# Hybrid RWKV-7 and Conformer layer on one core: the scan phase in the order of its source instead of the build's order

## The chip, the cores and the metric

The kernel runs on one core of a Trainium2 chip. The metric is the device time of one execution in microseconds (us). A kernel's time is the median of its runs; a profiled execution, taken by the hardware profiler, gives the trace from which all rows below come. The engines are TensorE (PE, with its weight loads listed apart as PEld), VectorE (DVE), ScalarE (ACT), GpSimd (POOL) and SyncE (SP), whose queue (SPq) issues the DMA transfers.

## What is computed

One layer works on 2048 latent tokens of 1024 channels, after a prefix of 256 context tokens. The normed and modulated input goes through one wide projection `w_in` and then through two branches, an RWKV-7 time mixing (16 heads of size 64, scanned forward and backward) and a Conformer convolution (31 taps), which are gated, added and projected:

```python
h = rmsnorm(x, norm_w) * (1.0 + scale[:, None]) + shift[:, None]
p = h @ w_in
prep = rwkv_prepare(rk, w0, w2, a0, a2, k_k, k_a)
y_sum, _, _ = rwkv_scans(prep, sc_f, sc_b)        # s = s*w + (s a) b + v k, forward and backward
y_a = rwkv_readout(y_sum, prep, r_k, lnx_w, lnx_b) * silu(g_a)
y_b = conformer_conv(glu, conv_w, conv_b, cln_w, cln_b) * silu(g_b)
merged = sigmoid(m_a) * (y_a @ w_proj_a) + sigmoid(m_b) * (y_b @ w_proj_b)
x_new = x + gate[:, None] * (merged @ w_out)
```

The layer's output goes through a last RMSNorm with `final_norm_w`.

## The kernel before, in words

The kernel has three phases. **Phase 1** (to about 1650 us of the span) makes `h`, projects the RWKV columns and part of the gates, and turns the recurrence into chunks of 64 tokens: for each chunk it stores small matrices (the inverse in `Tt`, the arrays `ar`, `bk`, `v`) in DRAM. Its last work is an `invert` on DVE, PE and ACT (L468 to L503).

The **scan phase** (L772 to the end of the loop over `g`) runs 8 pairs of heads x 9 steps x 4 chunks = 288 chunks, each for both directions. `chunk` (L989) is a chain: two matmuls `px` from the state `SV` and `arz` (PE), the copy `xs` (ACT), two matmuls `px` from `xs` and `Tt` (PE), the copy `UV` (ACT), `psy` from `UV` and `BK` (PE), and the next state `SV` (DVE, from `psy` and `pre`, which POOL makes). `outputs` (the matmuls `py`, then `y`) belongs to the chunk before. `prep` (L858) works for the next step: it loads `bk`, `ar`, `vvz`, `Tt`, and in pieces between the chunks it transposes (`pbk`, then `BK` on ACT; `pvt`, then `SV` and `UV` on ACT) and multiplies `psc` (PE), of which DVE makes `arz` and `sc`. `pbk`, `pvt`, the two `psc` and the readout's `pc` and `pv` share one PSUM pool, `pC`, of two buffers. `readout` normalizes finished rows and uses `Ln` and `Exp` on ACT.

Into the waits of this chain the source emits **filler**: `fill_gen` projects the columns of the gates and of the GLU in matmuls of 128x512 into `pg`, the products of the convolution run on DVE as chains of multiply-adds (`conv_gen`: `accq`, then `acc`), and, from chunk 236 on, `conv_branch` normalizes and projects (`pp`). How many fillers are emitted is decided by `until`, `conv_steps` and `pull`, from a model of the engines' clocks that the class `Clocked` (L789) keeps; it wraps PE, ACT and DVE, and so nearly all instructions of the scan carry the line of its call, L822. A filler's weights come through `load_w1` and `load_w2`: `load_w1` loads 512 KB of float32 into `wf` (L183; one buffer) and has ACT square it into `wjk` with the sum in `wss`; `load_w2` sums over partitions (`pf`, PE), makes a power of two from it (`p2f`, `p2t`, `p2x`, `p2s`, seven small instructions of DVE), and casts to `whi` (ACT) and `wlo` (DVE). In `fill_gen` the second half of one load, `second()`, and the first half of the next, `first()`, are called one after the other:

```python
def ahead(npr):
    if not w2:
        second()
    for _ in range(npr):
        yield from chore(prs.pop(0))
    first()
    yield
```

The **last phase** merges the branches, projects with `w_out` and writes the output.

In the whole kernel before, the build decides the order of instructions on every engine, and the order differs from that in which the source emits them. Each engine executes its instructions in the order that it gets. The parts of the code that the change touches are printed here.

Of the kernel before, what the change touches and what calls it, by code (L numbers as in the profile page):

```python
# [79 lines left out]
def kernel(ctx, tc, x, xT, cc, pp, w_in, w_mod, w_lora, w_pa, w_pb, w_out, fnw, bmg, out):  # L80
# [688 lines left out]
    s1.close()  # L769

    clk = dict(pe=0.0, dve=0.0, act=0.0, mode=0)
# [676 lines left out]
            pass  # L1451
    while "first" not in c_:
        next(cb, None)
    sb.close()

    c1 = pool(ctx, "c1", 1, "right")
# [146 lines left out]
```

## Time and profile before

| what | value |
|---|---|
| time, median of 3 runs | 4116.91 us (4113.39 to 4122.94) |
| the profiled execution | 4115.85 us |
| its span, first to last instruction | 4114.1 us |
| mean granted TensorE clock in it (share of full) | 0.966 |
| PE busy | 3802.2 us, 92% |
| DVE busy | 2950.5 us, 72% |
| ACT busy | 2181.7 us, 53% |

Busy time is time in which an engine executes; for PE it is no proof of full speed, since a slower clock makes each matmul longer. In a row such as `[1.30 <-ACT xs L822]` the engine had been idle for 1.30 us before the instruction, and what ended the idle time was ACT's instruction that writes `xs`. `128x512` are partitions x elements. A float32 matmul shows in the trace as two instructions, so that `x4` in a row of the timeline are two of the source. The rows of a timeline put several equal neighbours together (`x4`), with the time from the first's start to the last's end.

### The profile page before, as it was taken

Reading aid. Unit: us, or ns where it says so; the run is one execution under the profiler, and the core shown is the slowest. Engines: PE = TensorE matmul, PEld = TensorE weight load, DVE = VectorE, ACT = ScalarE, POOL = GpSimd, SP = SyncE. Lnnn points to the kernel's source line nnn. Section 1 sums busy time; section 2 is a strip of 40 time slices with the busy share of each in tenths; the row PEclk is TensorE's granted clock in tenths of the full one; section 3 lists DMA queues with packets and bytes.
Section 4 is the critical chain, followed back from the end, with each engine's and each line's share of the span. In section 5 each row is a group of like instructions: output and inputs, shape, how many; then the busy total and the mean of one; then the engine's idle time right before and its main releaser. Section 6 shows DMA issues by size and latency. Waiting matters only on the chain. (4 is left out here: it accounts for less than half of the span.)

```text
span 4114.1 us, 78249 instructions
## 1 busy us (share of the span) xinstructions
PE 3802.2 (92%) x29008; PEld 2254.8 (55%) x29008; DVE 2950.5 (72%) x7226; ACT 2181.7 (53%) x4356; POOL 356.8 (9%) x874
## 2 busy tenths in 40 slices
PE   7999999999999897999999999999999989898999
PEld 3444444444444443676666666666676655564444
DVE  5578788687778868768696869977765566754644
ACT  5666665666666554445445454455446546544522
POOL 0000000000000000111111111111111100010000
PEclk9999999999999999999999999999999999999999
DMA  5344443444444333444444433434554555546532
GB/s 205 127 165 144 157 162 134 140 149 157 146 150 162 134 137 115 92 81 115 88 107 96 113 87 82 124 86 104 118 125 116 139 160 126 148 107 203 163 101 75
DMA packets 586116, 528.68 MB, mean 129 GB/s; under 512 B 375044, under 2 KB 439940, under 8 KB 585224
## 3 DMA queue, kind: packets, MB, share of 16 engines
q1 hardware_dynamic: 585736, 523.68, 44.2%
q8 instruction: 231, 3.78, 0.4%
q14 instruction: 149, 1.22, 0.1%
HBM read 298.01 MB, written 196.35 MB: 120 GB/s over the span
## 5 line engine op out<-in xcount | busy, mean ns | idle before, releaser
L822 DVE SCALAR_TENSOR_TENSOR SV<-psy,PL,pre 64x64 f32<-64x64 f32 x1120 | 315.8, 282 | 187.7 <-PE psy L822 168.1
L1013 POOL TENSOR_SCALAR pre<-SV,PL 128x128 f32<-128x128 f32 x560 | 290.0, 518 | 1780.1 <-DVE SV L822 1708.0
L822 PE MATMUL pg<-hH,whi 128*128 128x512 f16 x864 | 336.1, 389 | 5.7 <-ACT whi L822 4.0
L822 PE MATMUL pg<-hH,wlo 128*128 128x512 f16 x864 | 335.6, 388 | 0.4 <-DVE wlo L822 0.3
L822 PE MATMUL pg<-hL,whi 128*128 128x512 f16 x864 | 335.8, 389 | 0.0
L822 DVE SCALAR_TENSOR_TENSOR acc<-z,cw,acc 128x512 f32<-128x512 f32 x464 | 331.7, 757 | 2.7
L212 PE MATMUL pg<-hH,whi 128*128 128x512 f16 x832 | 319.0, 385 | 4.7 <-ACT hH L282 4.5
L213 PE MATMUL pg<-hL,whi 128*128 128x512 f16 x832 | 319.7, 384 | 0.1
L214 PE MATMUL pg<-hH,wlo 128*128 128x512 f16 x832 | 319.2, 384 | 0.0
L822 ACT ACTIVATE xs<-px 128x256 f32<-128x256 f32 x288 | 109.3, 380 | 383.1 <-PE px L822 381.5
L822 PE MATMUL psc<-arz,bk 64*128 64x128 f32 (+1 forms) x2304 | 259.5, 293 | 14.7 <-ACT UV L822 7.1
L822 ACT ACTIVATE UV<-px 64x128 f32<-64x128 f32 x576 | 156.1, 271 | 211.7 <-PE px L822 207.0
L363 PE MATMUL pg<-hH,whi 128*128 128x512 f16 x672 | 259.9, 387 | 2.4 <-ACT whi L203 2.4
L363 PE MATMUL pg<-hL,whi 128*128 128x512 f16 x672 | 259.4, 386 | 0.0
L363 PE MATMUL pg<-hH,wlo 128*128 128x512 f16 x672 | 258.7, 385 | 0.7 <-DVE wlo L204 0.7
L822 PEld LDWEIGHTS <-whi 128*128 128x128 f16 x1728 | 172.8, 101 | 149.7 <-issue 20.2
L822 PEld LDWEIGHTS psc<-arz,bk 64*128 64x128 f32 x2304 | 211.7, 192 | 65.9 <-issue 13.3
L822 PE MATMUL px<-SV,arz 128*128 128x128 f32 x1152 | 222.8, 297 | 24.8 <-DVE SV L822 22.9
L822 PEld LDWEIGHTS px<-SV,arz 128*128 128x128 f32 x1152 | 181.9, 195 | 84.5 <-issue 29.3
L822 PE MATMUL psy<-UV,BK 128*128 128x128 f32 x1120 | 200.4, 300 | 25.6 <-ACT UV L822 23.2
L822 PE MATMUL px<-xs,Tt 128*128 128x128 f32 x1152 | 194.7, 292 | 29.4 <-ACT xs L822 28.3
L822 DVE TENSOR_TENSOR arz<-psc,msk 64x256 f32<-64x256 f32 x288 | 120.5, 419 | 140.7 <-PE psc L822 137.1
(376 smaller groups left out, 8704.2 us busy)
## 6 DMA issues: line engine op xcount, KB each, us to landing
wf<-in_w_in_dram SPq DMA_DIRECT2D x74, 512.0 KB, 3.8
arz<-arD SPq DMA_DIRECT2D x144, 256.0 KB, 4.9
bkD<-bk SPq DMA_DIRECT2D x64, 512.0 KB, 2.7
arD<-ar SPq DMA_DIRECT2D x64, 512.0 KB, 3.5
bk<-bkD SPq DMA_DIRECT2D x72, 256.0 KB, 3.8
bk<-bkD SPq DMA_DIRECT2D x144, 128.0 KB, 3.9
vvz<-vD SPq DMA_DIRECT2D x144, 128.0 KB, 2.9
lt<-loD SPq DMA_DIRECT2D x32, 512.0 KB, 4.9
```

The costliest lines, as they stand in the source:

```text
L212: PE.matmul(ps, whi[:, k, :], xhi(k), start=(k == 0), stop=False)
L213: PE.matmul(ps, whi[:, k, :], xlo(k), start=False, stop=False)
L214: PE.matmul(ps, wlo[:, k, :], xhi(k), start=False, stop=(k == NK - 1))
L363: PE.matmul(ps, wt[a][:, k, :], b[:, k, o:o + 512], start=(m == 0), stop=(m == 23))
L822: return fn(*a, **kw)
L1013: G.tensor_scalar(pr, SV[:, d, c, :], pl, 1.0, op0=ALU.mult, op1=ALU.mult)
```

## The change

From the start of the scan phase to the last chunk, the instructions of PE, ACT and DVE are issued in the order in which the source emits them. SP and POOL stay in the build's order, and so do all engines before and after. No instruction is added or removed by the source.

```diff
@@ -769,6 +769,9 @@
     s1.close()


+    order = ctx.enter_context(ExitStack())
+    order.enter_context(tc.manual_schedule(engines={mybir.EngineType.PE, mybir.EngineType.Activation, mybir.EngineType.DVE}))
+

@@ -1451,6 +1454,7 @@
     while "first" not in c_:
         next(cb, None)
+    order.close()
     sb.close()
```

Lines behind the first insertion move by 3: the line L822 of the call in `Clocked` is L825 in the changed kernel. What the change moves is shown at three places, by listings of the order in which an engine gets its instructions; numbers behind a name tell buffers apart.

ACT at a weight load in the middle of the scan (`f` belongs to a gate of the filler, `xs` and `UV<-px` to a chunk, `UV<-pvt` to `prep`), before:

```order
L822 ACTIVATE f_25514<-pg,un 128x512
L822 ACTIVATE xs<-px 128x256
L822 ACTIVATE UV<-pvt 64x4x64 x2
L822 ACTIVATE whi<-wf,p2s 128x1024
L822 ACTIVATE UV<-px 64x2x64 x2
L822 ACTIVATE wjk,wss<-wf 128x1024
L822 ACTIVATE xs<-px 128x256
```

and now, at the same load:

```order
L825 ACTIVATE f_25516<-pg,un 128x512
L825 ACTIVATE whi<-wf,p2s 128x1024
L825 ACTIVATE wjk,wss<-wf 128x1024
L825 ACTIVATE xs<-px 128x256
L825 ACTIVATE UV<-px 64x2x64 x2
L825 ACTIVATE UV<-pvt 64x4x64 x2
L825 ACTIVATE xs<-px 128x256
```

`wjk`, which reads the next tile's `wf`, now follows `whi` directly, and the `xs` and `UV` of the running chunk moved from ahead of them to behind them.

PE in a later chunk, where `prep` goes from `psc` of one direction to `pbk` of the next, before:

```order
L822 MATMUL px<-xs,Tt_18646 128x128 x2
L822 MATMUL psc<-arz_18649,bk 128x64 x8
L822 MATMUL psy<-UV,BK 128x128 x2
L822 LDWEIGHTS whi
L822 MATMUL pg<-hL,whi 128x512
L822 LDWEIGHTS wlo
L822 MATMUL pg<-hH,wlo 128x512
L822 LDWEIGHTS whi
L822 MATMUL pg<-hH,whi 128x512
L822 MATMUL pbk<-ident,bk 128x128 x4
L822 MATMUL pvt<-ident,vvz 128x128 x4
```

and now:

```order
L825 MATMUL px<-xs,Tt_18648 128x128 x2
L825 MATMUL psc<-arz_18651,bk 128x64 x8
L825 MATMUL pbk<-ident,bk 128x128 x2
L825 MATMUL psy<-UV,BK 128x128 x2
L825 MATMUL pbk<-ident,bk 128x128 x2
L825 MATMUL pvt<-ident,vvz 128x128 x4
L825 LDWEIGHTS whi
L825 MATMUL pg<-hL,whi 128x512
```

Two of the four `pbk` moved ahead of `psy` and directly behind `psc`, and the fillers `pg` that stood ahead of `pbk` now come after `pvt`.

ACT at the start of the scan (L588, L495 and L503 are phase 1), before:

```order
L588 ACTIVATE A_17786<-pA 32x256 x2
L822 ACTIVATE wjk,wss<-wf 128x1024
L822 ACTIVATE whi<-wf,p2s 128x1024
L822 ACTIVATE wjk,wss<-wf 128x1024
L822 ACTIVATE whi<-wf,p2s 128x1024
L822 ACTIVATE wjk,wss<-wf 128x1024
L822 ACTIVATE f_18941<-pg,un 128x512
L822 ACTIVATE whi<-wf,p2s 128x1024
L495 ACTIVATE DF<-pf 32x512 x2
L503 ACTIVATE A_17786<-pf 32x512 x2
L822 ACTIVATE wjk,wss<-wf 128x1024
```

and now, with all of phase 1 ahead of it:

```order
L825 ACTIVATE xs<-px 128x256
L825 ACTIVATE wjk,wss<-wf 128x1024
L825 ACTIVATE whi<-wf,p2s 128x1024
L825 ACTIVATE wjk,wss<-wf 128x1024
L825 ACTIVATE whi<-wf,p2s 128x1024
L825 ACTIVATE wjk,wss<-wf 128x1024
L825 ACTIVATE UV<-px 64x2x64 x2
L825 ACTIVATE xs<-px 128x256
```

The first weight loads moved from between the steps of the last `invert` to between the first chunk's `xs` and its `UV`.

## Rows read from the trace of the kernel before

**Rows 1.** The page's first part: busy time, share of the span, instructions of each engine.

```profile
PE 3802.2 (92%) x29008; PEld 2254.8 (55%) x29008; DVE 2950.5 (72%) x7226; ACT 2181.7 (53%) x4356; POOL 356.8 (9%) x874
```

**Rows 2.** Groups of instructions, 1680 to 3750 us: busy, mean ns | idle before, releaser.

```profile
L822 PE MATMUL px<-SV,arz 128*128 128x128 f32 x1148 | 222.0, 297 | 24.8 <-DVE SV L822 22.9 <-DVE arz L822 0.2
...
L822 PE MATMUL psy<-UV,BK 128*128 128x128 f32 x1120 | 200.4, 300 | 25.6 <-ACT UV L822 23.2
L822 PE MATMUL px<-xs,Tt 128*128 128x128 f32 x1152 | 194.7, 292 | 29.4 <-ACT xs L822 28.3
...
L822 PE MATMUL pbk<-ident,bk 128*128 128x128 f32 x568 | 93.6, 280 | 24.5 <-DVE sc L822 23.8 <-DVE arz L822 0.3
```

**Rows 3.** Timeline of ACT at one weight load: start, us, instruction, [idle before <-releaser].

```profile
2347.49 0.37 ACT L822 ACTIVATE xs<-px 128x256 f32<-128x256 f32 x1
...
2350.80 1.15 ACT L822 ACTIVATE whi<-wf,p2s 128x1024 f16<-128x1024 f32 x1 [2.15 <-DVE p2s L822]
2352.08 0.56 ACT L822 ACTIVATE UV<-px 64x128 f32<-64x128 f32 x2
2357.71 1.06 ACT L822 ACTIVATE wjk<-wf 128x1024 f16<-128x1024 f32 x1 [5.08 <-DMA wf<-in_w_in_dram]
```

**Rows 4.** Timelines of DVE and of SP's queue at the same load.

```profile
2351.98 1.28 DVE L822 SCALAR_TENSOR_TENSOR wlo<-wf,p2s,whi 128x1024 f16<-128x1024 f32 x1 [1.22 <-ACT whi L822]
...
2353.42 0.56 SPq L183 DMA_DIRECT2D wf<-in_w_in_dram  x1
```

**Rows 5.** Timeline of ACT at the first weight loads of the scan.

```profile
1618.83 1.15 ACT L822 ACTIVATE whi<-wf,p2s 128x1024 f16<-128x1024 f32 x1 [4.47 <-DVE p2s L822]
1625.01 1.06 ACT L822 ACTIVATE wjk<-wf 128x1024 f16<-128x1024 f32 x1 [5.04 <-DMA wf<-in_w_in_dram]
...
1629.26 1.15 ACT L822 ACTIVATE whi<-wf,p2s 128x1024 f16<-128x1024 f32 x1 [3.10 <-DVE p2s L822]
1635.28 1.06 ACT L822 ACTIVATE wjk<-wf 128x1024 f16<-128x1024 f32 x1 [4.87 <-DMA wf<-in_w_in_dram]
```

**Rows 6.** Timeline of PE at the same loads.

```profile
1614.40 0.38 PE L822 MATMUL pf<-wss,ones 128*128 128x1 f32 x2 [3.00 <-ACT wjk L822]
1626.21 0.59 PE L822 MATMUL pf<-wss,ones 128*128 128x1 f32 x2 [11.43 <-ACT wjk L822]
```

**Rows 7.** Timeline of PE at the load of rows 3.

```profile
2346.42 0.28 PE L822 MATMUL pf<-wss,ones 128*128 128x1 f32 x2
...
2351.43 0.61 PE L822 MATMUL px<-xs,Tt 128*128 128x128 f32 x4
...
2353.61 0.38 PE L822 MATMUL pg<-hL,whi 128*128 128x512 f16 x1
...
2355.77 0.71 PE L822 MATMUL px<-SV,arz 128*128 128x128 f32 x4
...
2359.32 0.71 PE L822 MATMUL px<-xs,Tt 128*128 128x128 f32 x4 [1.30 <-ACT xs L822]
```

**Rows 8.** Timeline of ACT at the first chunk of the scan.

```profile
1679.62 0.38 ACT L822 ACTIVATE xs<-px 128x256 f32<-128x256 f32 x1 [2.86 <-PE px L822]
1680.81 0.56 ACT L822 ACTIVATE UV<-px 64x128 f32<-64x128 f32 x2 [0.80 <-PE px L822]
```

**Rows 9.** The tile pbk, 1680 to 3750 us: PE's idle time before it, times.

```profile
  DVE sc L822: 23.8, 19
```

**Rows 10.** Timeline of DVE: seven conv steps of one chain, and of two.

```profile
2055.39 5.48 DVE L822 SCALAR_TENSOR_TENSOR accq<-z,cw,accq 128x512 f32<-128x512 f32 x7
...
1903.50 4.84 DVE L822 SCALAR_TENSOR_TENSOR acc<-z,cw,acc 128x512 f32<-128x512 f32 x7
```

**Rows 11.** Groups of instructions, 1680 to 3750 us: ACT's table loads.

```profile
L822 ACT ACT_TABLE_LOAD x68 | 87.2, 1283 | 1.2
```

**Rows 12.** Timeline of PE behind a long wait.

```profile
3415.70 1.22 PE L822 MATMUL px<-xs,Tt 128*128 128x128 f32 x4 [4.12 <-ACT xs L822]
```

**Rows 13.** The stretch behind it: busy us of each engine, PEclk, DMA share, GB/s.

```profile
core 0: us, PE busy (x) PEld busy (x) DVE busy (x) ACT busy (x) POOL busy (x), PEclk, DMA share, GB/s
...
3415.70:3422.40 6.70, 6.70 (x28) 4.46 (x29) 6.56 (x19) 6.66 (x13) 0.00 (x0) 0.51 0.17 33
```

## The prediction, made before the changed kernel had run

> **What bounds the kernel now.** I read the page's busy times first: TensorE (PE) works 92% of the span, VectorE (DVE) 72%, ScalarE (ACT) 53% [rows 1]. So PE sets the time, and what the change is worth is PE's idle time that it removes or adds. Then I grouped instructions by what ended the idle time before them, in the scan (1680 to 3750 us). PE's largest idle groups there are small: 29.4 us before `px<-xs,Tt`, 25.6 before `psy`, 24.8 before `px<-SV,arz`, 24.5 before `pbk` [rows 2], 104 us in 2070. The scan is a chain (px, xs, px, UV, psy, SV) with filler matmuls `pg` packed into its waits, and the build packs them well. The question is therefore whether the source's order packs as well; the order listings say where it doesn't, and the trace gives prices.
>
> **The change, part by part.** Nothing is added or removed in arithmetic; three instruction streams are ordered otherwise from the start of the scan to the last chunk. On PE the two orders are nearly the same chunk by chunk (fillers per chunk too, after the start). Five places differ.
>
> *1. Weight loads on ACT (the term that decides).* A weight tile goes `pf` (PE), the small pow2 steps and then `whi` (ACT), `wlo` (DVE), the transfer of the next `wf` (SP; one buffer, so it waits for `whi` and `wlo`), `wjk` (ACT). In the source `second()` and `first()` follow each other, so that in the new order `wjk` stands directly behind `whi` in 41 of 43 loads of the scan; the build does that in the first three and puts 1 to 12 other ACT instructions between them in the rest. Now ACT stops at `wjk` until the transfer has landed, and xs or UV of the running chunk stands behind it. At the load of the first listing, in the trace, xs of that chunk ran at 2347.49, ahead of `whi` at 2350.80; `whi` ended 2351.95, `wlo` began 2351.98 (1.28), the transfer was issued at 2353.42 (0.56), and `wjk` began 2357.71 [rows 3, 4]: 5.76 us, of which some 3.7 are the landing. How long the whole circle takes where nothing stands between `whi` and `wjk` the trace shows at the start of the scan, where the build has the source's arrangement: ACT waits 5.04 and 4.87 us for the transfer [rows 5], and from `pf` to the end of the following `wjk` there are 1614.40 to 1626.07, 11.7 us, and 1626.21 to 1636.34, 10.1 us [rows 5, 6]. With the accumulator read behind `wjk` (the next `pf` began 0.14 after it) and xs (0.37, [rows 3]), a matmul that needs xs comes some 10.6 us after `pf`. What PE has in between is fixed by the new order: counted over the 41 loads, with 0.216 us for a filler (ten from 2353.61 to 2355.77, [rows 7]) and 0.22 to 0.3 for the others, it is 5.0 us on average (1.1 to 11.1). For the load of the listing: `pf` at 2346.42, the matmul that needs xs at 2351.43 [rows 7], so 5.0 us are covered and 5.6 are not. Three of the 41 belong to the start (part 2). **38 x 5.6 = 213 us.** Ends: if half of the 3.10 us goes for which ACT waited for the pow2 steps of the second circle [rows 5], since they are no longer mixed with other DVE work, 38 x 4.1 = 156; if the circle is that of the first of the two, 38 x 7.2 = 274. I take 213, since in the second circle there is less DVE work. A part was paid already: the next `px` in the trace waited 1.30 us for xs [rows 7]; that goes into part 6.
>
> *2. The start.* The build runs 144 filler matmuls (31 us of PE) and the first three weight loads beside the last `invert` on DVE, 1614 to 1650. In the new order all of them stand behind the first px. The scan may begin earlier: first xs at 1679.62 now [rows 8], some 1664 then, as DVE is relieved of some 6 us and SP's loads move up. But ACT's new order is xs, `wjk`, `whi`, `wjk`, `whi`, `wjk`, UV: two circles at about 10 us each, so first UV at about 1687 instead of 1680.81. With 31 us of fillers to do later: 6 + 31, I take **+40** (25 if the start comes earlier, 50 if a transfer is late).
>
> *3. `pbk` right behind `psc`.* It needs a PSUM buffer that DVE frees with arz and sc. In the new order 72 `psc` groups have `pbk` next, in the old 27; elsewhere `psy` and fillers stood between. Where the wait shows in the trace it is 23.8 us in 19 cases, 1.25 each [rows 9]. 45 more x 1.25 = **56 us**; ends 0 (DVE there already) and 90 (2 us each, with a conv step of 0.78 ahead [rows 10]). `psy`, on the chain, waits behind it.
>
> *4. Conv steps on DVE.* The build mixes two independent chains, seven steps in 4.84 us; a single chain takes 5.48, so 0.69 and 0.78 a step [rows 10]. Some 460 `acc` steps: 41 us of DVE, which has 28% idle [rows 1]. I take **+20**, from 0 to 41.
>
> *5. Table loads.* 39 instead of 71 in the scan: 32 x 1.283 us [rows 11] = 41 us of ACT, most of it where xs waits. **-30**, ends 0 and -41.
> The Trainium skill (ScalarE: Activation LUTs, What ACT_TABLE_LOAD costs) puts a switch at 1283 ns and a drain of about 1380 ns: 2.66 us, and by that 85 us would go, which speaks for the change. By it the term would be some -62 and the time 4393, an estimate. The row agrees with the 1283, and no row here shows the drain, so I stay with the row.
>
> *6. Clock and catch-up.* Behind an idle of 4.12 us before a `px` [rows 12] the granted clock was 0.51 for 6.7 us [rows 13], that is the 1.2 GHz level: up to 3.3 us of PE time. With 38 new idles of that kind: 0 to 125; I take 1 us each, **+40**, as low stretches of now go where their idles go. For waits of now that the new ones swallow [rows 2]: **-30**.
>
> Sum: 40 + 213 + 56 + 20 - 30 + 40 - 30 = 309. The profiled execution took 4115.85 us, a microsecond under the median of the three runs, 4116.91: 4425 us.
>
> **The rivals.**
> (a) *Milder.* PE runs so far behind that ACT's stop costs little: transfers land in 3 us, pow2 runs at once, and a late chunk is made good with fillers. For it: 1.30 us was all that the example cost [rows 7]. Against it: in the new order no filler stands ahead of the waiting matmul beyond those counted. Loads at 2 us, 76 instead of 213, clock 10, `pbk` 25: 4116 + 40 + 76 + 10 + 25 + 20 - 30 - 30 = 4227.
> (b) *Heavier.* DVE stops too (`wlo` waits for `whi`, and arz and SV stand behind it), and every stop brings the slow clock: 274 for loads, 125 for the clock, `pbk` 56: 4116 + 40 + 274 + 125 + 56 + 20 - 30 - 30 = 4571. For it: the slow clock behind the idle shown [rows 12, 13]. Against it: idles of a microsecond are common now, and PE's mean clock is high nevertheless.
> The Trainium skill (TensorE: Matmul & The Clock Gate, What's actually happening) has the array throttled unless activity releases it; the row of that idle agrees, and by the rule every new idle threatens a slow stretch, as this rival says.
> (c) *Faster.* The build's order mixes ACT work of later chunks ahead of the chain; the source's order puts the chain first. Half of the 104 us of idle and 30 us of table loads go: 4116 - 52 - 30 + 40 = 4074, if a load costs PE nothing. It decides where a load costs PE less than (52 + 30 - 40)/38 = 1.1 us, i.e. where xs follows `pf` within 6.1 us instead of 10.6. For it: ACT is idle half of the time. Against it: `whi` (1.15), `wlo` (1.28), issue (0.56) and landing (3.7) make 6.7 alone [rows 3, 4], and twice the circle was measured at over 10 [rows 5, 6].
> (d) *Nothing happens.* The listings show all three streams changed; only a sum that cancels would give it, 4117.
>
> **How the numbers follow.** Forecast 0.52 (4310 to 4520), (a) 0.2, (b) 0.18, (c) 0.08, (d) 0.02. The range 4190 to 4580 leaves out (c), (d) and the tails of (a) and (b). About 0.2% is what a measurement of this kernel can tell from no change; slower by more than that 0.9, faster 0.08, within 0.02.
>
> **What would show it.** Right: in the changed profile ACT has some 200 us of idle before `wjk` ended by the transfer of `wf` (now 5 us in the example), xs and UV follow it, and PE's idle before `px<-xs` and `psy<-UV` grows from 55 to over 200 us; `pbk` waits for sc rise to some 80; the first chunks take 7 us each; table loads fall by 32; the mean clock falls below 0.95. Wrong: idle before `wjk` large but PE's idle not (a), DVE idle before `wlo` and a clock at 0.9 (b), or PE's idle below that of now (c).

## The result, and the profile after

The changed kernel takes 4703.58 us (median of 4 runs, 4699.69 to 4709.07), the kernel before beside it 4115.15 us: a ratio of 1.1428, 95% interval 1.1407 to 1.1449. The forecast was slower, by 309 us to 4425, with a range up to 4580. The direction was right; the loss is 588 us, nearly twice the forecast and outside the range.

The profiled execution took 4709.07 us. Its page, with the busy times that answer to [rows 1]:

```profile
span 4707.3 us, 78279 instructions
...
PE 3896.6 (83%) x29008; PEld 2334.0 (50%) x29008; DVE 3014.2 (64%) x7226; ACT 2142.0 (46%) x4324; POOL 372.4 (8%) x874
```

PE's busy time rose by 94 us (3802.2 to 3896.6) with the same 29008 matmuls, and its idle time, span less busy, from 312 to 811 us, by 499. Together that is the whole difference of the spans, 593 us. Where it lies shows in the two kernels cut at the same places of the program: the end of phase 1, the `xs` of chunk 24, of chunk 228 and of the last chunk, the end. First the kernel before (columns: busy time of each engine in the stretch, PEclk the granted clock, DMA share, GB/s):

```profile
core 0: us, PE busy (x) PEld busy (x) DVE busy (x) ACT busy (x) POOL busy (x), PEclk, DMA share, GB/s
0.00:1640.00 1640.00, 1497.14 (x14708) 711.04 (x14709) 1233.92 (x3118) 997.95 (x1602) 63.33 (x287) 0.96 0.43 149
1640.00:1811.40 171.40, 165.03 (x1289) 121.46 (x1288) 130.99 (x292) 74.46 (x198) 31.59 (x57) 1.00 0.44 89
1811.40:3253.00 1441.60, 1348.73 (x8725) 958.54 (x8724) 1096.55 (x2658) 723.41 (x1671) 210.83 (x416) 0.97 0.45 105
3253.00:3744.50 491.50, 445.86 (x2719) 306.90 (x2717) 297.20 (x733) 252.00 (x584) 51.02 (x115) 0.94 0.54 140
3744.50:4114.10 369.60, 345.42 (x1574) 156.87 (x1574) 191.87 (x428) 133.92 (x302) 0.00 (x0) 0.97 0.40 130
```

and now the changed kernel:

```profile
0.00:1640.00 1640.00, 1493.69 (x14670) 709.05 (x14670) 1230.86 (x3090) 991.05 (x1592) 63.02 (x287) 0.96 0.42 149
1640.00:1877.20 237.20, 171.21 (x1317) 127.36 (x1318) 85.19 (x241) 80.74 (x206) 23.05 (x53) 0.82 0.31 67
1877.20:3737.10 1859.90, 1427.94 (x8740) 1024.69 (x8739) 1197.67 (x2733) 694.12 (x1649) 233.81 (x420) 0.87 0.34 83
3737.10:4328.90 591.80, 454.14 (x2706) 313.75 (x2705) 308.54 (x736) 244.01 (x584) 52.55 (x114) 0.88 0.44 117
4328.90:4707.30 378.40, 349.57 (x1581) 159.12 (x1579) 191.94 (x428) 132.10 (x296) 0.00 (x0) 0.96 0.37 123
```

Phase 1 and the last phase are as they were. The start of the scan costs 66 us more (237.2 against 171.4), the 204 chunks after it 418 (1859.9 against 1441.6), chunks 228 to the last 100. In the middle stretch 79 of the 418 are busy time of the same matmuls: the granted clock fell from 0.97 to 0.87 of full. That is the level of 1.2 GHz taken more often: between 1640 us and the last chunk the clock was low in 95 stretches, 709 us together, against 23 with 143 us before.

The groups of instructions of the changed kernel's scan, with the idle time before them and what ended it, answer to [rows 2, 11]:

```profile
L825 PE MATMUL pg<-hH,whi 128*128 128x512 f16 x864 | 352.1, 407 | 61.1 <-ACT whi L825 33.2 <-ACT f L825 27.4 <-DVE p2f L825 0.5
...
L825 PE MATMUL psc<-arz,bk 64*128 64x128 f32 x2272 | 228.8, 311 | 132.2 <-ACT UV L825 111.7 <-ACT sqy L825 20.5
...
L825 PE MATMUL psy<-UV,BK 128*128 128x128 f32 x1120 | 212.7, 320 | 51.4 <-ACT UV L825 51.3
L825 PE MATMUL px<-SV,arz 128*128 128x128 f32 x1148 | 210.1, 304 | 41.8 <-DVE SV L825 39.4
L825 PE MATMUL px<-xs,Tt 128*128 128x128 f32 x1148 | 200.0, 301 | 86.6 <-ACT xs L825 86.0
...
L825 PE MATMUL pbk<-ident,bk 128*128 128x128 f32 x568 | 112.2, 305 | 121.7 <-DVE sc L825 99.9 <-DVE arz L825 21.8
...
L825 ACT ACT_TABLE_LOAD x36 | 46.2, 1283 | 0.6
L825 ACT ACTIVATE wjk<-wf 128x1024 f16<-128x1024 f32 x43 | 45.4, 1056 | 221.6 <-DMA wf<-in_w_in_dram 136.6 <-DMA wf<-in_w_pb_dram 47.0 <-DMA wf<-in_w_pa_dram 38.1
...
L825 PE MATMUL pf<-wss,ones 128*128 128x1 f32 x86 | 15.4, 248 | 42.9 <-ACT wjk L825 42.9
...
L825 PE MATMUL pfs<-s__37040,ones 128*128 128x1 f32 x2 | 0.6, 362 | 23.4 <-DVE s__37040 L825 23.4
```

and three groups of the kernel before that were not shown ahead of the prediction:

```profile
L822 PE MATMUL psc<-arz,bk 64*128 64x128 f32 x2272 | 255.1, 293 | 14.7 <-ACT UV L822 7.1 <-ACT sqy L822 5.7 <-PE pf L822 1.0
...
L822 ACT ACTIVATE wjk<-wf 128x1024 f16<-128x1024 f32 x39 | 41.1, 1053 | 25.3 <-DMA wf<-in_w_in_dram 14.1 <-DMA wf<-in_w_pa_dram 6.5 <-DMA wf<-in_w_pb_dram 4.5
...
L822 PE MATMUL pf<-wss,ones 128*128 128x1 f32 x80 | 13.7, 240 | 7.9 <-ACT wjk L822 7.8
```

ACT now stands idle for 221.6 us before `wjk`, ended by the transfer of `wf`, where it was 25.3. PE's idle rose before `px<-xs,Tt` from 29.4 to 86.6, before `psy` from 25.6 to 51.4, before `pf` from 7.9 to 42.9 and before the first filler of a new tile (`pg<-ACT whi`) to 33.2: 151 us that hang on weight loads, 83 of them before `px<-xs,Tt` and `psy`. `pbk` went from 24.5 to 121.7. And `psc`, of which the prediction says nothing, went from 14.7 to 132.2, nearly all of it behind the UV copies. `pfs`, four instructions in the whole scan that belong to `conv_branch`, wait 42 us together, one of them 23.4.

The load of the first listing, which the prediction worked out at 5.6 us, in the changed kernel (ACT, then PE):

```profile
2563.20 1.15 ACT L825 ACTIVATE whi<-wf,p2s 128x1024 f16<-128x1024 f32 x1 [0.56 <-DVE p2s L825]
2569.23 1.06 ACT L825 ACTIVATE wjk<-wf 128x1024 f16<-128x1024 f32 x1 [4.88 <-DMA wf<-in_w_in_dram]
...
2570.28 0.36 ACT L825 ACTIVATE xs<-px 128x256 f32<-128x256 f32 x1
...
2561.75 0.28 PE L825 MATMUL pf<-wss,ones 128*128 128x1 f32 x2
...
2570.70 0.81 PE L825 MATMUL px<-xs,Tt 128*128 128x128 f32 x4 [3.77 <-ACT xs L825]
```

The mechanism is there: `wjk` behind `whi`, 4.88 us of waiting for the transfer, and xs of the chunk behind both, for which PE waits 3.77 us. At this load the circle is shorter than the 10.6 us taken: from `pf` at 2561.75 to the waiting `px` at 2570.70 are 8.95, since `whi` begins 1.45 us after `pf`. It is the shortest of all loads; another one (PE and ACT, in order of time) takes 13.07:

```profile
2030.37 0.28 PE L825 MATMUL pf<-wss,ones 128*128 128x1 f32 x2
...
2034.44 1.15 ACT L825 ACTIVATE whi<-wf,p2s 128x1024 f16<-128x1024 f32 x1 [1.67 <-issue]
2041.80 1.06 ACT L825 ACTIVATE wjk<-wf 128x1024 f16<-128x1024 f32 x1 [6.21 <-DMA wf<-in_w_in_dram]
...
2043.44 1.22 PE L825 MATMUL psy<-UV,BK 128*128 128x128 f32 x4 [8.72 <-ACT UV L825]
```

What was missed is seen in a chunk that makes the `psc` of a step's second direction (PE, then ACT):

```profile
2414.61 0.48 PE L825 MATMUL psc<-arz,bk 64*128 64x128 f32 x2
2415.98 1.16 PE L825 MATMUL psc<-arz,bk 64*128 64x128 f32 x14 [0.89 <-ACT UV L825]
...
2414.71 0.55 ACT L825 ACTIVATE UV<-px 64x128 f32<-64x128 f32 x2 [0.90 <-PE px L825]
2415.17 0.76 ACT L825 ACTIVATE UV<-pvt 64x256 f32<-64x256 f32 x2
```

`psc` stands directly behind `px`. Its two outputs take the buffers of `pC` that `pbk` and `pvt` had; the second is free only when ACT has copied `pvt` to SV and UV, and those UV copies stand in ACT's new order behind the `UV<-px` of the chunk. In the source `prep` is cut into pieces, and `pieces` emits two of them in a gap: for the second direction the UV copies and `psc` fall into one gap, for the first one `psc` and the first half of the next `pbk`. In the source's order both pairs run one directly behind the other. The wait comes 70 times.

### The profile page after: what moved, and what is told of

The parts are those of the page before. It is cut to its first block, busy times and chain, and to the rows that moved or that the text cites. A ratio compares the mean times of both kernels' runs of the same rounds, so it can differ in the third digit from the quotient of the medians.

```text
span 4707.3 us, 78279 instructions
## 1 busy us (share of the span) xinstructions
PE 3896.6 (83%) x29008; PEld 2334.0 (50%) x29008; DVE 3014.2 (64%) x7226; ACT 2142.0 (46%) x4324; POOL 372.4 (8%) x874
## 5 line engine op out<-in xcount | busy, mean ns | idle before, releaser
L1016 POOL TENSOR_SCALAR pre<-SV,PL 128x128 f32<-128x128 f32 x560 | 306.0, 547 | 2350.6 <-DVE SV L825 2343.2
L825 DVE SCALAR_TENSOR_TENSOR SV<-psy,PL,pre 64x64 f32<-64x64 f32 x1120 | 316.8, 283 | 264.9 <-PE psy L825 245.1
L825 PE MATMUL pg<-hH,whi 128*128 128x512 f16 x864 | 352.1, 407 | 61.1 <-ACT whi L825 33.2
L825 DVE TENSOR_TENSOR arz<-psc,msk 64x256 f32<-64x256 f32 x288 | 120.1, 417 | 380.3 <-PE psc L825 351.0
L825 DVE SCALAR_TENSOR_TENSOR acc<-z,cw,acc 128x512 f32<-128x512 f32 x464 | 349.0, 752 | 15.4
L825 PE MATMUL pg<-hL,whi 128*128 128x512 f16 x864 | 351.7, 407 | 0.0
L825 PE MATMUL pg<-hH,wlo 128*128 128x512 f16 x864 | 350.2, 405 | 1.1 <-DVE wlo L825 1.1
L825 PE MATMUL psc<-arz,bk 64*128 64x128 f32 (+1 forms) x2304 | 234.1, 313 | 134.3 <-ACT UV L825 113.8
L212 PE MATMUL pg<-hH,whi 128*128 128x512 f16 x832 | 319.5, 385 | 4.1 <-ACT hH L282 4.0
L213 PE MATMUL pg<-hL,whi 128*128 128x512 f16 x832 | 320.0, 385 | 0.0
L214 PE MATMUL pg<-hH,wlo 128*128 128x512 f16 x832 | 319.5, 384 | 0.0
L825 ACT ACTIVATE xs<-px 128x256 f32<-128x256 f32 x288 | 108.6, 377 | 452.4 <-PE px L825 451.6
L825 PEld LDWEIGHTS <-whi 128*128 128x128 f16 x1728 | 183.1, 106 | 225.3 <-issue 65.6
L825 PEld LDWEIGHTS psc<-arz,bk 64*128 64x128 f32 x2304 | 187.7, 209 | 180.6 <-ACT UV L825 128.0
L825 PE MATMUL px<-xs,Tt 128*128 128x128 f32 x1152 | 201.2, 302 | 86.6 <-ACT xs L825 86.0
L363 PE MATMUL pg<-hH,whi 128*128 128x512 f16 x672 | 260.3, 387 | 2.5 <-ACT whi L203 2.4
L825 ACT ACTIVATE UV<-px 64x128 f32<-64x128 f32 x576 | 155.9, 271 | 228.8 <-PE px L825 224.4
L363 PE MATMUL pg<-hL,whi 128*128 128x512 f16 x672 | 259.8, 387 | 0.0
L363 PE MATMUL pg<-hH,wlo 128*128 128x512 f16 x672 | 259.4, 386 | 0.3 <-DVE wlo L204 0.3
L825 PE MATMUL psy<-UV,BK 128*128 128x128 f32 x1120 | 212.7, 320 | 51.4 <-ACT UV L825 51.3
L825 PE MATMUL px<-SV,arz 128*128 128x128 f32 x1152 | 211.3, 305 | 42.7 <-DVE SV L825 40.3
L825 PEld LDWEIGHTS px<-SV,arz 128*128 128x128 f32 x1152 | 191.6, 208 | 105.9 <-issue 48.2
```

Source lines behind the costliest of these rows:

```text
L212: PE.matmul(ps, whi[:, k, :], xhi(k), start=(k == 0), stop=False)
L213: PE.matmul(ps, whi[:, k, :], xlo(k), start=False, stop=False)
L214: PE.matmul(ps, wlo[:, k, :], xhi(k), start=False, stop=(k == NK - 1))
L363: PE.matmul(ps, wt[a][:, k, :], b[:, k, o:o + 512], start=(m == 0), stop=(m == 23))
L825: return fn(*a, **kw)
L1016: G.tensor_scalar(pr, SV[:, d, c, :], pl, 1.0, op0=ALU.mult, op1=ALU.mult)
```

## The experiments

Four theories were held against each other. **A**, the prediction's: ACT's stop at `wjk` is the larger part. **B**: PE's own order is, with `psc` and `pbk` put where their buffers are not free. **C**: VectorE's order holds back the chain. **D**, formed after the first four runs: a sum of waits of like size, each of them an instruction that the source emits directly behind what it needs. **E** and **F** stand with the runs that test them. Each comparison is with a run of the kernel before on the same chip (4106 to 4117 us); the 19 runs of the kernel before in the last experiments lie between 4102.9 and 4122.3 us, so that where there was one run of each, differences under 20 us mean little.

### One engine at a time

The four kernels differ from the changed one in the set of engines alone:

```diff
-    order.enter_context(tc.manual_schedule(engines={mybir.EngineType.PE, mybir.EngineType.Activation, mybir.EngineType.DVE}))
+    order.enter_context(tc.manual_schedule(engines={mybir.EngineType.Activation}))
```

Only ScalarE (e1_act):

> Only ScalarE issues in the source's order, TensorE and VectorE are left to the build. Theory A (ScalarE standing at wjk until the next weight tile has landed is the larger part of the loss): ScalarE's idle time before wjk stays near the 220 us of the changed kernel and the time is 4300 to 4450 us. Theory B (TensorE's own order, with psc and pbk put where their PSUM buffer is not yet free, is the larger part): the build finds other work for TensorE, psc and pbk wait as in the kernel before, and the time stays under 4250 us.

Only TensorE (e2_pe):

> Only TensorE issues in the source's order. Theory A: idle before wjk falls back to some 25 us, the time is 4150 to 4250 us. Theory B: psc waits for the UV copies by some 100 us and pbk for sc by some 100 us as in the changed kernel, and the time is 4300 to 4450 us.

Only VectorE (e3_dve):

> Only VectorE issues in the source's order. Theories A and B: within 40 us of the kernel before, 4115 to 4155 us (the single conv chain costs some 20 us). Theory C (VectorE's order holds back SV, arz and sc behind conv steps and wlo): over 4200 us, with px waiting for SV by 60 us or more.

TensorE and VectorE (e4_pe_dve):

> TensorE and VectorE in the source's order, ScalarE left to the build. Theory A: over half of the 590 us goes, 4200 to 4400 us. Theory B: less than half goes, 4420 to 4600 us, with psc and pbk waiting by some 200 us together.

| in the source's order | time, us | above the kernel before (4116.14) | PE busy, us (before: 3802.2) | PE idle, us (before: 311.9) |
|---|---|---|---|---|
| ScalarE | 4322.94 | +207 | 3907.1 | 414.1 |
| TensorE | 4373.56 | +257 | 3773.2 | 598.7 |
| VectorE | 4304.63 | +188 | 3899.6 | 403.3 |
| TensorE and VectorE | 4412.53 | +296 | 3762.4 | 648.4 |

Each engine alone costs 190 to 260 us. ScalarE's own order gives A's wait before `wjk` in full, by the groups of e1_act:

```profile
L825 PE MATMUL psy<-UV,BK 128*128 128x128 f32 x1120 | 205.8, 304 | 15.3 <-ACT UV L825 13.4
L825 PE MATMUL px<-xs,Tt 128*128 128x128 f32 x1148 | 200.5, 298 | 17.0 <-ACT xs L825 15.5
...
L825 ACT ACTIVATE wjk<-wf 128x1024 f16<-128x1024 f32 x42 | 44.4, 1057 | 249.6 <-DMA wf<-in_w_in_dram 161.8 <-DMA wf<-in_w_pb_dram 46.3 <-DMA wf<-in_w_pa_dram 41.5
```

and the time is where A put it, but not by A's path: PE waits less for xs and UV than in the kernel before (32 us against 55), presumably because the build gives PE other work meanwhile. What grew is `pf` behind `wjk`, from 7.9 to 71.8 us, and PE's busy time, by 105 us. And A has TensorE alone at 4150 to 4250 and VectorE alone near 4135, and both are far above. B fails on e1_act, which should have stayed under 4250. Its waits are partly there with TensorE alone (groups of e2_pe):

```profile
L825 PE MATMUL psc<-arz,bk 64*128 64x128 f32 x2272 | 178.2, 291 | 23.1 <-ACT sqy L825 23.1
...
L825 PE MATMUL pbk<-ident,bk 128*128 128x128 f32 x568 | 112.5, 305 | 132.7 <-DVE sc L825 126.7 <-DVE arz L825 6.0
```

`pbk` waits 132.7 us, more than in the changed kernel, but `psc` does not wait for UV: ACT is left to the build there, which puts the copies in time. With ScalarE alone in the source's order `psc` waits 19.8 us in all, 0.6 of it for UV. So the `psc` wait belongs to two engines' orders together. ACT's wait before `wjk` in e2_pe did not fall to 25 us either, but to 83.8. C's number holds for e3_dve (over 4200), its sign does not: `px<-SV` has 24.0 us of idle time ahead of it, as before. The sign comes in e4_pe_dve, with 74.7 us, 71.3 of them for SV: this wait, too, needs two engines' orders. With one engine's order fixed, the build also orders the other engines otherwise: `psc` stands in 242 groups in the kernel before, in 325 in e1_act and in 300 in e3_dve (its same 2272 matmuls are busy for 255.1, 310.9 and 295.5 us), and about half of what these two kernels lose is PE's busy time. With TensorE and VectorE in the source's order half of the loss is left, 296 of 588: just above A's 4400 and just under B's 4420, so that it decides for neither; `psc` and `pbk` wait 148 us together there, under B's 200. These runs do not isolate an engine's share; they show that no engine's order is harmless and that none is the cause by itself.

### One wait at a time

`wjk` is taken away from its place behind `whi` (e5_wjk). The transfer is issued where it was; the square goes into a list and is emitted behind the second `UV<-px` from there, or by the next `load_w2`, whichever comes first:

```diff
-        S.activation(jk, wf, AF.Square, accum_out=ss)
+        def square():
+            o = jk if jk is not None else fp.tile([P, NK, P], F16, name="wjk", tag="f5", bufs=4)
+            S.activation(o, wf, AF.Square, accum_out=ss)
+        if hi is None:
+            sq_wait.append([2, square])
+        else:
+            square()
...
```

> The changed kernel, with wjk emitted two chunks behind the transfer that it reads (or at the next pf, if that comes first) instead of directly behind whi. Theory A (weight loads are over half of the loss): 4300 to 4450 us. Theory D (the loss is a sum of waits of like size: loads 160 us, psc behind the UV copies 114, pbk behind arz and sc 122, the start 66, the stretch from chunk 228 on 100, slow clock 95): ScalarE's idle time before wjk falls from 222 to under 60 us, and the time is 4500 to 4590 us.

The time is 4528.41 us, 422 above the kernel before instead of 588: 166 us are gone. The waits that should go went (groups of e5_wjk):

```profile
L843 PE MATMUL px<-xs,Tt 128*128 128x128 f32 x1152 | 191.1, 291 | 13.7 <-ACT xs L843 12.8
...
L843 ACT ACTIVATE wjk<-wf 128x1024 f16<-128x1024 f32 x42 | 44.3, 1055 | 18.0 <-DMA wf<-in_w_pa_dram 9.7 <-DMA wf<-in_w_in_dram 4.8 <-DMA wf<-in_w_pb_dram 2.8
```

ACT's wait before `wjk` fell from 221.6 to 18.0, PE's before `px<-xs` from 86.6 to 13.7 and before `psy` from 51.4 to 15.1: 109 us of idle time, and PE's busy time fell by 67. What did not go are the waits of `pf` for `wjk` (46.1) and of a tile's first filler for `whi` (34.8). A's number, under 4450, is missed; D's is met.

The pieces of `prep` are cut otherwise (e6_pieces), so that neither pair shares a gap:

```diff
-                if c in PB:
+                if c in PB and d == 0:
                     yield
...
-                yield
+                if x is UV or d == 0:
+                    yield
...
             yield
+            if d == 0:
+                yield
         st[g] = dict(ar=ar, sc=sc, BK=BK, UV=UV, SV=SV)
```

> The changed kernel, with the pieces of prep cut otherwise: psc no longer in one gap with the UV copies ahead of it or with pbk behind it. Theory A: 4600 us or more. Theory D: psc waits for UV and pbk waits for sc and arz fall by 150 us or more together, part comes back as a wait of px for arz, and with the clock the time is 4440 to 4550 us.

4508.94 us, 403 above the kernel before: 185 us are gone, and by their groups in e6_pieces these were the waits:

```profile
L825 PE MATMUL psc<-arz,bk 64*128 64x128 f32 x2272 | 180.9, 296 | 20.5 <-ACT sqy L825 20.5
...
L825 PE MATMUL pbk<-ident,bk 128*128 128x128 f32 x568 | 98.7, 302 | 55.7 <-DVE sc L825 38.3 <-DVE arz L825 16.9
```

`psc` waits for UV no longer, `pbk` lost 66 of 121.7 us. Together 178 us of waits went; `px` waits 19 us longer for SV and `psy` 22 longer for UV in exchange. PE's busy time fell by 75 us, 48 of them in `psc` itself (228.8 to 180.9). This settles the part that the prediction lacked: a cut of the pieces that changes nothing in the work is worth as much here as the term on which the prediction rested.

The source's order only in the middle (e7_window):

```diff
+            if cnt["n"] == 24:
+                order.enter_context(tc.manual_schedule(engines={mybir.EngineType.PE, mybir.EngineType.Activation, mybir.EngineType.DVE}))
...
                 for _ in fill:
                     pass
+                order.close()
```

> The changed kernel, with the source's order only from chunk 24 to chunk 236; the build orders the start and the part with conv_branch. Theory D: chunk 24 is reached near 1811 us as in the kernel before and the part behind chunk 236 costs as before, so 4540 to 4600 us. Theory A: the same, since the loads lie between: it tells only what the two ends cost.

4518.86 us, 412 above the kernel before and 21 under what D expected: the two ends cost 176, about the 166 of the stretches above. Chunk 24 begins at 1806.7 (1811.4 before), and from chunk 228 to the last there are 494 us (491 before, 592 in the changed kernel).

All three edits (e8_all):

> The edits of the three kernels ahead of this one together. Theory D: the gains add up, 4200 to 4350 us, still above the kernel before. Theory E (the source's order is as good as the build's once these waits are out): 4100 to 4180 us.

4220.53 us, 114 above the kernel before: 474 of 588 us are gone, where the three alone gave 166 + 185 + 176 = 527. The time is in D's range, though the gains fall 53 us short of adding up; E falls. What is left shows in the groups of e8_all:

```profile
L842 PE MATMUL pg<-hH,whi 128*128 128x512 f16 x809 | 316.4, 391 | 60.4 <-ACT whi L842 30.6 <-ACT f L842 29.4 <-DVE p2f L842 0.2
...
L842 PE MATMUL pbk<-ident,bk 128*128 128x128 f32 x568 | 92.2, 285 | 52.2 <-DVE sc L842 41.4 <-DVE arz L842 10.4
...
L842 PE MATMUL pf<-wss,ones 128*128 128x1 f32 x80 | 13.1, 233 | 38.6 <-ACT wjk L842 33.0 <-DMA Tt<-TB 5.5
```

Against the kernel before `pbk` has 28 us more idle time ahead of it, `pf` 31, the first filler of a tile and the filler behind `f` 59 together, `px<-SV` 15 and `psc` 12, and `px<-xs` and `psy` have 22 less. PE's whole idle time from 1640 us to the last chunk is 280 us against 145; less the 25 us by which PE is busy for less, that is about the 114. These waits look to be of the same kind (`pf` behind `wjk`, a filler behind the `whi` that it reads), but edits that take them away were not tried.

### The same edits in the build's order

To see whether the edits are worth something by themselves, each was made in the kernel before, with all engines in the build's order, and timed in 10 runs against 19.

> The kernel before, all engines in the build's order, with the pieces of prep cut as in e6_pieces. Theory D: psc and pbk wait little there already (7.6 and 24.5 us), so the edit brings between -25 and +15 us, against some 195 in the source's order. Theory F (the edit is worth something by itself, whoever sets the order): 100 us or more faster.

> The kernel before, all engines in the build's order, with wjk emitted two chunks later as in e5_wjk. Theory D: ScalarE waits only some 25 us before wjk there, so between -25 and +15 us, against some 175 in the source's order. Theory F: 100 us or more faster.

The cut of the pieces gives 4103.31 us against 4110.58, ratio 0.9983 (0.9967 to 0.9999): 7 us, under 0.2%, which the interval just sets off from nothing. (`psc` waits 14.7 us in the kernel before, not the 7.6 of the text above.) The later `wjk` gives 4112.68, ratio 1.0004 (0.9991 to 1.0016): nothing. The 185 and 166 us are the price of those places in the source's order; the build orders round them by itself. F falls.

### The convolution's chain

The two halves of the accumulation are emitted in turn (e10_conv):

```diff
-            for e, x, nt in ((0, z[:, 0, b:b + w + 1], n0), (1, z1, n1)):
-                o = acc[:, :, e]
-                for j in range(nt):
+            for j in range(n0):
+                for e, x, nt in ((0, z[:, 0, b:b + w + 1], n0), (1, z1, n1)):
+                    if j < nt:
+                        o = acc[:, :, e]
...
```

> The changed kernel, with the two halves of the convolution's accumulation emitted in turn, so that no step follows its own result. The step falls from some 0.78 to 0.69 us. Theory D: VectorE is not the bound, 4680 to 4705 us. Theory C (VectorE's order holds back the chain): 4600 us or less.

4674.56 us, 564 above the kernel before instead of 588: 24 us, from one run, just under D's figure and far from C's. The same with VectorE alone in the source's order (e12_dve_conv):

> Only VectorE in the source's order, as in e3_dve, with the convolution's two halves emitted in turn as in e10_conv. Theory C (the single conv chain is what VectorE's order costs): 4200 us or less. Theory D (the conv steps are worth some 30 us, as in e10_conv, and the rest comes from the order that the build then gives TensorE and from conv_branch): 4260 to 4300 us.

4270.24 us, 158 above the kernel before instead of 188. C, by which it should be 4200 or less, falls again, and D's 4260 to 4300 holds. In both runs the `acc` steps are 29 us shorter with their idle time (364.4 to 335.8 us in e10_conv). What makes VectorE's order alone cost 158 us beside the conv steps stays open in its cause: PE is busy for 72 us more than in the kernel before, 28 of them in `psc`, and its idle time rose by 82, in groups of under 20 us each.

## Why the prediction was right in direction and wrong in size

The step that failed is the sentence "Five places differ": the sum put the wait of `psc` behind the UV copies at nothing (it rose by 118 us), and the part with `conv_branch` too. Of the terms that it had, `pbk`, the start and the clock were sized too low and the weight loads too high.

1. **Weight loads, 213 us.** The mechanism is shown. In the changed kernel's trace `wjk` stands directly behind `whi` in 41 of 43 loads, as counted, and behind each of these PE comes to wait: 21 times for xs, 8 times for UV, 10 times with the next `pf` for `wjk` itself, twice with `psc`. Taking it away gave 166 us (e5_wjk), PE's busy time among it. The size was off. In the 38 loads behind the start these waits come to 157 us, 4.1 each instead of 5.6. The circle was not too long: from `pf` to the matmul that waits there are 11.7 us in the mean (8.95 to 16.9) where 10.6 were taken, and `whi` follows `pf` by 3.4 (1.4 to 5.8). What was sized too low is the time that PE fills meanwhile: 7.6 us in the mean instead of 5.0, of which 6.0 are work and the rest other waits. That the 157 is the text's lower end of 156 is luck, since its reason, faster pow2 steps, did not come: 3.4 us against the 3.05 of the circle that it took. Against the kernel before, idle groups that hang on loads rose by 151 us; only the 83 before `px<-xs` and `psy` are the stop that the text describes, the others are `pf` and a tile's first filler, which e5_wjk left.

2. **The start, 40 us.** It cost 66. The first xs did not move up: DVE is relieved, but the last `invert` ends no earlier on PE (1655.23 us; before 1652.86), and PE then waits 7.17 us for the transfer of `bk` and 3.46 for that of `vvz`. And the first UV came at 1698.98 instead of some 1687 (PE, then ACT, of the changed kernel):

```profile
1643.62 1.92 PE L492 MATMUL pf<-DF,A 32*32 32x32 f32 x64 [29.89 <-DVE DF L482]
...
1662.40 1.09 PE L825 MATMUL pbk<-ident,bk 128*128 128x128 f32 x4 [7.17 <-DMA bk<-bkD]
...
1679.56 0.38 ACT L825 ACTIVATE xs<-px 128x256 f32<-128x256 f32 x1 [4.18 <-PE px L825]
...
1688.94 1.06 ACT L825 ACTIVATE wjk<-wf 128x1024 f16<-128x1024 f32 x1 [5.00 <-DMA wf<-in_w_in_dram]
...
1698.98 0.54 ACT L825 ACTIVATE UV<-px 64x128 f32<-64x128 f32 x2
```

The two circles took some 9 us each, and began behind an xs at 1679.56 instead of at 1664. The text also overlooked the clock here. With the fillers gone from beside the last `invert` PE stands idle for 29.89 us, and the granted clock is at its lower level until 1704 us, where the kernel before has it full (before, then changed):

```profile
1643.60:1704.00 60.40, 59.07 (x563) 37.32 (x563) 36.22 (x73) 21.83 (x50) 7.91 (x13) 1.00 0.45 90
...
1643.60:1704.00 60.40, 26.15 (x333) 20.64 (x334) 8.27 (x30) 15.54 (x30) 3.60 (x7) 0.50 0.40 88
```

The 64 matmuls of an `invert` step take 1.92 us there, as shown, where they took 1.20.

3. **`pbk` behind `psc`, 56 us.** Its idle time rose by 97. The number of places was right, the price was not (the tile `pbk` in the changed kernel):

```profile
  DVE sc L825: 99.9, 64
  DVE arz L825: 21.8, 7
```

71 waits of 1.71 us, where [rows 9] gave 1.25. With TensorE alone in the source's order it is as much (e2_pe: 132.7 us), so DVE's new order is not needed for the longer wait; what makes it longer wasn't tested. It lay just outside the end of 90.

4. **Conv steps, 20 us.** 24 and 31 us in the two runs that took it away, one run each: it fits.

5. **Table loads, -30 us.** They fell by 32, from 68 to 36 in the scan, as the listing said. No gain is to be seen: the waits for xs, where it should have shown, rose for other reasons. Whether the table loads alone are worth something wasn't tried.

6. **Clock 40, catch-up -30.** PE's busy time for the same matmuls rose by 94. That is a net figure: `psc` alone is busy for 26 us less (255.1 to 228.8), as it stands in 144 groups instead of 242, so that the other matmuls took some 120 more. Low stretches went from 23 to 95, where the text took as many to come as to go. Catch-up can't be told apart here; with the stop at `wjk` taken away (e5_wjk) the waits for xs and UV are 26 us under those of the kernel before.
The Trainium skill (TensorE: Matmul & The Clock Gate, What's actually happening) says that the default is the throttled state and activity releases it; the rows agree, with 0.87 where PE was idle for 432 of 1859.9 us and 0.97 where it was idle for 93 of 1441.6.

7. **What the sum lacked.** "Five places differ" is the sentence that failed. The sixth is `psc` behind the UV copies: 118 us more idle time, and 185 with `pbk` and PE's busy time when both pairs were parted. The listing of the PE place shows `psc` directly behind `px` in both orders; whether ACT has freed its buffer by then is decided by ACT's order, and I read the listing for `pbk` alone. Nor had the part with `conv_branch` a term: chunks 228 to the last cost 100 us more, `pfs` 38 of it.

As a sum of the idle groups in the scan: loads 151, `pbk` 97, `psc` 118, `pfs` 38, fillers behind `f` 27, `px<-SV` 17, small ones 22, together 470; the time before 1680 us 24, the last phase 5, PE's busy time 94: the 593. The loads were forecast 62 us too high; all else together was forecast at 96 us and came to 442.

Of the rivals, (b) was nearest with 4571: its second half, the slow clock behind every stop, came with its signs (DVE's idle time before `wlo` rose from 10.7 to 49.9 us, the mean clock fell to 0.907), and 94 of its 125 us. Its first, loads at 274, was not. Of the forecast's own signs ACT's idle time before `wjk`, `pbk`, the table loads and the clock came; PE's idle time before `px<-xs` and `psy` grew from 55 to 138 us and not to over 200. (c) fell: with the load's stop, both pairs and the two ends taken out, the source's order is still 114 us behind (e8_all).

## What to carry to other kernels

A source that was written for a scheduler may hand an engine an instruction directly behind the one that it waits for, on another engine; the scheduler moves it, an in-order stream stops at it, with everything that is queued behind. Before an engine is put into the source's order, go through every place where an instruction follows its producer, its buffer's last reader included, and not only through the one with the longest wait: here some 140 waits of one or two microseconds cost as much as 40 of four. An engine's idle time is no measure of the loss by itself: with ScalarE alone in the source's order ACT stood 249.6 us before `wjk`, and PE waited less for xs and UV than before.

## What the runs showed of the hardware

The clock's share was larger than expected. From 1640 us to the last chunk the granted clock was at its lower level (1.2 GHz) for 709 us, against 143 us in the kernel before, while waits of 1 to 10 us were spread over the scan. With the waits most of it went: 218 us in e8_all.

Busy time is not the clock's alone. In e8_all PE is busy for 3776.9 us, less than the 3802.2 of the kernel before, at a lower mean clock (0.959 against 0.966). The order counts too: the same 2272 matmuls `psc` of 64x128 are busy for 178.2 us where they stand in 144 groups (e2_pe), for 255.1 in 242 (the kernel before) and for 310.9 in 325 (e1_act), at 290 to 293 ns each in all three, so that in the trace they overlap more where more of them stand together.

The transfers did not suffer: the 74 loads of `wf` from `w_in` landed in 3.6 us in the median, against 3.8 before.
